# The MLP's second product by seven block products over pairs of k-tiles, and a phase table by Sin

## The chip, the cores and the metric

The program runs on one core of a Trainium2 chip. Its engines are TensorE (PE in the profile; the loading of its stationary operand is PEld), VectorE (DVE), ScalarE (ACT), GpSimd (POOL) and SyncE (SP), which here only issues DMAs. The metric is the device time of one execution in microseconds (us); lower is better. A measurement is the median of several executions.

## The reference

Two layers, each a token mixer with cross-attention into 256 memory tokens, and an MLP, with a layer norm behind each; 1024 tokens of width 1024. Layer 0 mixes by a gated delta rule, layer 1 by S5, a diagonal state-space layer. All inputs are float32. What the change touches is the MLP of both layers and a small table of S5:

```
f = jnp.square(jax.nn.relu(x @ mlp_w1[i])) @ mlp_w2[i]          # (1024,1024)@(1024,4096), then @(4096,1024)
x = layer_norm(DN_ALPHA * x + f, ln2_g[i], ln2_b[i])
...
abar_re, abar_im = mag * jnp.cos(a_im * dt), mag * jnp.sin(a_im * dt)   # S5: powers of these turn by a_im*dt each step
```

## The kernel before, in words

**Numbers.** A float32 factor is split into two parts of type fp32r: `hi`, a cast by ScalarE, and `lo`, the rest, a subtraction by VectorE (`split`, L528 for the subtraction). A product is three matmuls, hi·hi, hi·lo, lo·hi (`mm3`, L351 to L353), each 128 x 128 stationary against 512 moving columns into a PSUM bank.

**First product of the MLP** (`mlp_first`, `mlp_pair`). It is already done in blocks: the 32 tiles of 128 hidden units are taken as 16 pairs, tokens, inner dimension and the pair each halved, and seven block products (of 12 matmuls) replace eight, with sums before and behind. Their sums end in four hidden blocks of 128 units x 512 tokens per pair; `hidden` applies relu and square on ScalarE and stores the block in DRAM (`hd`). Operands of pair n+1 are made while pair n is multiplied (`mlp_weights`); their buffers have tags h1 to h5 with 5 to 9 slots each, and a split part waits until TensorE has left its slot.

**Second product** (`mlp_second`). Eight groups of four hidden tiles. A group loads and splits 4 tiles of hidden values (L676) and 4 of `w2` (L528), and then makes 16 blocks of 128 tokens x 512 columns; a block is 12 matmuls in a row into one bank (`tm`), and is added to `y` in SBUF (L698; by a ScalarE copy in the first group). Three banks take turns. In group 4 the residual is added (L702). In the last group each finished row of `y` gets its layer norm (`done`).

**S5's tables.** While layer 0's MLP runs, `side` does work that layer 1 will need, in steps `fb` 0 to 12: steps 1 to 4 make two of eight phase tables each (`s5_tables`, L1530, by doubling the range of angles seven times), and steps 5 to 12 each make two sets of matrices (`s5_mats`: on VectorE L1570 to L1572, on TensorE `pz` and `pg`). Steps 0 to 6 stood in the first product, 7 to 12 in the second.

**S5's front** (`s5_front`) is layer 1's mixer with its attention: `S` makes scores and their softmax, `T` transposes them, `V` multiplies by the values. Scores went to the banks `pi` and `sc`, one each.

**What sets the order.** At the end of tracing, `settle` lays the whole program out anew: it walks through all instructions with a price for each, due times from TensorE's row, and the slots of every tag, and fixes the order on each engine. A row that is late holds everything behind it on its engine.

## Time and profile before

| | |
|---|---|
| median of 3 runs | 2709.89 us (2707.24 to 2713.09) |
| profiled execution | 2711.34 us, its span 2709.6 us |
| TensorE busy | 2645.0 us, 98% of the span |
| VectorE busy | 1779.6 us, 66% |
| ScalarE, GpSimd busy | 1223.6 us and 355.9 us |
| data moved by DMA | 367.89 MB, mean 136 GB/s |
| layer 0, first product | from about 911 to 1172 us (some of it begins earlier) |
| layer 0, second product | from 1172 to about 1557 us |
| layer 1, first product, with the norm before it | about 2055 to 2350 us |
| layer 1, second product and end | about 2350 to 2709.6 us |

The span is the time from the first to the last instruction. A matmul's row shows its own duration; matmuls overlap, so durations do not add up to time. A row `start, duration, engine line op out<-in [idle <-releaser]` of a timeline names in brackets how long the engine had stood idle and what it then waited for. A row of windows gives, for a stretch, each engine's busy time with its instructions (x), the clock granted to TensorE (1.00 is full), and the DMA engines' share and rate.

### The profile page before, as it was taken

Reading aid. Unit: us, or ns where it says so; the run is one execution under the profiler, and the core shown is the slowest. Engines: PE = TensorE matmul, PEld = TensorE weight load, DVE = VectorE, ACT = ScalarE, POOL = GpSimd, SP = SyncE. Lnnn points to the kernel's source line nnn. Section 1 sums busy time; section 2 is a strip of 40 time slices with the busy share of each in tenths; the row PEclk is TensorE's granted clock in tenths of the full one; section 3 lists DMA queues with packets and bytes.
Section 4 is the critical chain, followed back from the end, with each engine's and each line's share of the span. In section 5 each row is a group of like instructions: output and inputs, shape, how many; then the busy total and the mean of one; then the engine's idle time right before and its main releaser. Section 6 shows DMA issues by size and latency. Waiting matters only on the chain.

```text
span 2709.6 us, 36841 instructions
## 1 busy us (share of the span) xinstructions
PE 2645.0 (98%) x13085; PEld 2183.8 (81%) x13085; DVE 1779.6 (66%) x3474; ACT 1223.6 (45%) x2773; POOL 355.9 (13%) x525
## 2 busy tenths in 40 slices
PE   8999999999999999999999999989999999999998
PEld 6888787888887788777777888878887888888887
DVE  6675757575769799746585766663768555535647
ACT  6666665654436544452222145553235545522210
POOL 1111212110003012201110122211011000000002
PEclk9999999999999999999999999999999999999999
DMA  5434444444423355463343186655323332533411
GB/s 197 130 118 124 125 113 120 122 134 139 152 78 132 123 164 165 148 208 120 128 146 120 70 247 195 194 183 179 121 71 131 107 117 101 194 113 127 154 63 62
DMA packets 233848, 367.89 MB, mean 136 GB/s; under 512 B 94224, under 2 KB 110816, under 8 KB 233664
## 3 DMA queue, kind: packets, MB, share of 16 engines
q1 hardware_dynamic: 212032, 308.40, 35.6%
q0 software_dynamic: 19328, 52.94, 6.5%
q10 hardware_dynamic: 2304, 4.20, 0.4%
q8 instruction: 103, 1.69, 0.3%
q14 instruction: 81, 0.66, 0.1%
HBM read 255.87 MB, written 109.54 MB: 135 GB/s over the span
## 4 chain that ended last, share of the span: by engine, by line
PE 76%; DVE 10%; ACT 5%; issue 3%; DMA 3%; POOL 1%; SPq 0%; POOLq 0%; ACTq 0%; DVEq 0%
PE tm L351 11%; PE tm L353 11%; PE tm L352 11%; PE pB L351 3%; PE pB L353 3%; PE pB L352 3%; PE iv L1035 2%; PE pC L351 2%; PE pC L353 2%; PE pC L352 2%; PE wi L353 2%; PE wi L351 2%; PE wi L352 2%; PE pA L351 2%; PE pA L353 2%
## 5 line engine op out<-in xcount | busy, mean ns | idle before, releaser
L351 PE MATMUL tm<-w2h,hk 128*128 128x512 f32 x1024 | 400.5, 391 | 0.0
L353 PE MATMUL tm<-w2h,hk 128*128 128x512 f32 x1024 | 399.4, 390 | 0.0
L352 PE MATMUL tm<-w2l,hk 128*128 128x512 f32 x1024 | 399.3, 390 | 0.0
L698 DVE TENSOR_TENSOR y<-tm,y 128x512 f32<-128x512 f32 x224 | 154.1, 688 | 212.4 <-PE tm L353 212.0
L527 ACT CAST w2h<-w2r 128x512 fp32r<-128x512 f32 x128 | 78.7, 621 | 375.3 <-PE tm L353 297.4
L351 PEld LDWEIGHTS tm<-w2h,hk 128*128 128x128 f32 x1024 | 192.2, 188 | 40.3 <-DVE y L698 0.3
L353 PEld LDWEIGHTS tm<-w2h,hk 128*128 128x128 f32 x1024 | 192.2, 188 | 39.9
L352 PEld LDWEIGHTS tm<-w2l,hk 128*128 128x128 f32 x1024 | 192.3, 188 | 39.3
L351 PE MATMUL wi<-xTh,wih 128*128 128x512 f32 x384 | 157.8, 411 | 0.0
L353 PE MATMUL wi<-xTh,wil 128*128 128x512 f32 x384 | 152.9, 398 | 0.0
L352 PE MATMUL wi<-xTl,wih 128*128 128x512 f32 x384 | 152.3, 397 | 0.0
L466 POOL TENSOR_SCALAR mv<-mv 128x1 f32<-128x1 f32 x32 | 26.2, 819 | 898.3 <-DVE mv L465 659.4
L1410 DVE TENSOR_TENSOR y<-tm,y 128x512 f32<-128x512 f32 x128 | 87.9, 688 | 59.5 <-PE tm L353 57.6
L528 DVE TENSOR_TENSOR w2l<-w2r,w2h 128x512 fp32r<-128x512 f32 x128 | 87.2, 689 | 50.9 <-PE tm L352 26.4
L676 DVE TENSOR_TENSOR hk<-hr,hk 128x512 fp32r<-128x512 f32 x128 | 83.4, 683 | 20.6 <-ACT hk L675 20.2
L353 PEld LDWEIGHTS wi<-xTh,wil 128*128 128x128 f32 x384 | 72.5, 189 | 13.9
L351 PEld LDWEIGHTS wi<-xTh,wih 128*128 128x128 f32 x384 | 72.8, 189 | 12.7 <-ACT qT L861 0.4
L352 PEld LDWEIGHTS wi<-xTl,wih 128*128 128x128 f32 x384 | 72.8, 190 | 12.3 <-issue 0.3
L535 ACT ACTIVATE u<-u 128x512 f32<-128x512 f32 x64 | 40.4, 631 | 89.2 <-DVE u L622 70.2
L675 ACT CAST hk<-hr 128x512 fp32r<-128x512 f32 x128 | 71.1, 617 | 14.7 <-DMA hr<-hd 13.1
L351 PE MATMUL tm<-ow,ok 128*128 128x512 f32 x160 | 63.5, 397 | 0.0
L353 PE MATMUL tm<-ow,ok 128*128 128x512 f32 x160 | 62.5, 391 | 0.0
(507 smaller groups left out, 7168.8 us busy)
## 6 DMA issues: line engine op xcount, KB each, us to landing
w2r<-in_w_dram SPq DMA_DIRECT2D x128, 256.0 KB, 3.5
hr<-hd SPq DMA_DIRECT2D x60, 512.0 KB, 4.5
w1r<-in_w_dram SPq DMA_DIRECT2D x40, 512.0 KB, 3.7
w1r<-in_w_dram SPq DMA_DIRECT2D x64, 256.0 KB, 4.5
hd<-u SPq DMA_DIRECT2D x64, 256.0 KB, 2.0
wir<-in_w_in_dram SPq DMA_DIRECT2D x24, 512.0 KB, 3.8
or<-in_w_o_dram SPq DMA_DIRECT2D x24, 512.0 KB, 3.4
or<-cat SPq DMA_DIRECT2D x24, 512.0 KB, 3.3
```

Of the source, the lines that this page charges most:

```text
L351: mm(ps, a[0], b[0], start=start, stop=False, skip_group_check=onto)
L352: mm(ps, a[0], b[1], start=False, stop=False, skip_group_check=onto)
L353: mm(ps, a[1], b[0], start=False, stop=stop, skip_group_check=onto)
L466: nc.gpsimd.tensor_scalar(mv[:, 2:3], mv[:, 1:2], 1e-5, None, op0=ALU.add)
L527: nc.scalar.copy(hi, s)
L528: nc.vector.tensor_tensor(lo, s, f32(hi), op=ALU.subtract)
L535: nc.scalar.activation(x, x, AF.Relu)
L675: nc.scalar.copy(hi, s)
L676: nc.vector.tensor_tensor(lo, s, f32(hi), op=ALU.subtract)
L698: nc.vector.tensor_tensor(o, ps, o, op=ALU.add)
L1035: nc.tensor.matmul(ps[:, t, :], a[:, t, :], b[:, t, :], start=True, stop=True)
L1410: nc.vector.tensor_tensor(y[c], ps, y[c], op=ALU.add)
```

## The change

**The second product.** Of the 16 pairs of hidden tiles, 14 are now multiplied in seven block products instead of eight: token halves by the pair's two tiles, the tiles by column halves. `mlp_round` takes 4, 5 and 5 pairs at once: for each of seven products in turn, it goes through the round's pairs and for each pair through four banks (`self.sets`, two sets of four that take turns), three matmuls per bank. Four of the products are added onto what the product two before left in the same banks; after each product the four banks are added to quarters of `y` (L755, L757), after the first to `x1` (L743, L745), which is added to three quarters at the end (L684). The last two pairs keep the old form (`mlp_last`).

**What that asks for.** The sums of hidden blocks are made once, in the first product (`hidden_sums`, L556, four per pair), and stored, so `hd` has seven blocks per pair. The sums of `w2` blocks are made in place (`source`, L693, four per pair). Each product of each pair splits both of its factors (`operand`, L764 for the subtraction).

**S5.** A phase table is now a remainder of turns, step times frequency, put through Sin on ScalarE; `s5_phases` shrinks accordingly. Steps 0 to 7 of the side work stand in the first product and 8 to 12 in the second, where the matrices use the bank set that is not in use. In `s5_front` the last scores go to the two `mm` banks, and `T` and `U` change places twice.

```diff
+SEVEN = 14
+SIDE = {3: 8, 7: 9, 10: 10, 14: 11, 17: 12}
...
-    def hidden(self, f, h, x):
+    def hidden(self, n, b, x):
 
...
-        nc.sync.dma_start(self.hd[f][:, h * HALF:(h + 1) * HALF], o)
+        nc.sync.dma_start(self.hd[n, b], o)
+        return o
+
+    def relu2(self, x):
+        self.nc.scalar.activation(x, x, AF.Relu)
+        self.nc.scalar.activation(x, x, AF.Square)
+
+    def hidden_sums(self, n, A11, A12, A21, A22):
+
+        if n >= SEVEN:
+            return
+        V = self.nc.vector
+        if A11 is None:
+            A11 = self.tile("h4", [P, HALF], F32, "hid")
+            self.nc.sync.dma_start(A11, self.hd[n, 0])
+        for b, o, x, z, op in ((3, A22, A21, A22, ALU.add), (5, A21, A11, A21, ALU.subtract),
+                               (4, A11, A22, A11, ALU.subtract), (6, A12, A12, A11, ALU.subtract)):
+            V.tensor_tensor(o, x, z, op=op)
+            self.nc.sync.dma_start(self.hd[n, b], o)
 
...
+        kept = []
+
         def second():
             if 1 in O:
                 go(2, a, False)
-                self.hidden(2 * n, 0, a)
+                kept.append(self.hidden(n, 0, a))
...
-        self.hidden(2 * n + 1, 1, u3)
+        self.hidden(n, 2, u3)
 
         def rest():
             go(3, c, False)
             V.tensor_tensor(u2, c, u2, op=ALU.add)
-            self.hidden(2 * n, 1, u2)
+            self.hidden(n, 3, u2) if n >= SEVEN else self.relu2(u2)
             go(4, b, False)
             V.tensor_tensor(p1, b, p1, op=ALU.add)
-            self.hidden(2 * n + 1, 0, p1)
+            self.hidden(n, 1, p1)
+            self.hidden_sums(n, kept[0] if kept else None, p1, u2, u3)
 
         held.append(rest)
 
...
-            if side and n % 2 == 0 and n:
-                side(n // 2 - 1)
+            for fb in {2: (0,), 4: (1,), 6: (2,), 8: (3,), 10: (4,), 11: (5,), 13: (6,), 15: (7,)}.get(n, ()) if side else ():
+                side(fb, ("pa",) * 4)
         self.finish(held)
...
     def mlp_second(self, i, xd, done, side):
 
...
+        self.sets = [("mm", "mm", "pi", "po"), ("pa", "pa", "pa", "sc")]
+        acc = {}
+        n0 = 0
+        for r, g in enumerate((4, 5, 5)):
+            self.mlp_round(i, r, range(n0, n0 + g), xd, acc, side)
+            n0 += g
+            self.sets.reverse()
+        y, x1 = acc["y"], acc["x1"]
+        for q in (1, 2, 3):
+            for t in range(4):
+                o = self.quarter(y, q, t)
+                self.nc.vector.tensor_tensor(o, o, x1[:, t], op=ALU.add)
+        self.mlp_last(i, y, done)
+
+    def quarter(self, y, q, t):
+        return y[4 * (q // 2) + t][:, (q % 2) * HALF:(q % 2 + 1) * HALF]
+
+    def mlp_round(self, i, r, pairs, xd, acc, side):
+        nc = self.nc
+        V = nc.vector
+        sub = lambda o, x, z: V.tensor_tensor(o, x, z, op=ALU.subtract)
+        L, R = slice(0, HALF), slice(HALF, 2 * HALF)
+        w2 = lambda n, q, o: nc.sync.dma_start(o, self.a["w2"][i, 2 * n + q])
+        r1, r2, t2 = self.quad(F32, "wr"), [], []
+        for j, n in enumerate(pairs):
+            if j == 4:
+                r1.append(self.tile("raw", [P, 1024], F32, "wr"))
+            w2(n, 0, r1[j])
+
+        def source(m, j, n):
+            if m == 1:
+                return r1[j][:, L]
+            if m == 6:
+                r2.append(self.tile("w1" if j < 4 else "raw", [P, 1024], F32, "wr"))
+                w2(n, 1, r2[j])
+                sub(r1[j][:, L], r1[j][:, R], r1[j][:, L])
+                t2.append(acc["x1"][:, 4 + j] if j < 4 else self.tile("h4", [P, HALF], F32, "t2"))
+                sub(t2[j], r2[j][:, R], r1[j][:, L])
+                return t2[j]
+            if m == 7:
+                sub(r1[j][:, R], r2[j][:, R], r1[j][:, R])
+                return r1[j][:, R]
+            if m == 4:
+                sub(r2[j][:, L], r2[j][:, L], t2[j])
+            return {2: r2[j][:, L], 5: r1[j][:, L], 4: r2[j][:, L], 3: r2[j][:, R]}[m]
+
+        left = {1: 0, 2: 1, 3: 6, 4: 2, 5: 3, 6: 4, 7: 5}
+        into = {1: None, 6: 1, 2: 0, 7: 3, 5: 3, 4: 2, 3: 1}
+        held = {}
+        for at, m in enumerate((1, 6, 2, 7, 5, 4, 3)):
+            own, onto = at % 2, m in (2, 7, 4, 3)
+            if not onto:
+                held[own] = [self.psum(t, f"q{m}") for t in self.sets[own]]
+            bank = held[own]
+            for j, n in enumerate(pairs):
+                s = self.tile("h3", [P, HALF], F32, "hr")
+                nc.sync.dma_start(s, self.hd[n, left[m]])
+                h = self.operand(s, "hk")
+                w = self.operand(source(m, j, n), "wk")
+                for t in range(4):
+                    c = slice(t * P, (t + 1) * P)
+                    self.mm3(bank[t], (h[0][:, c], h[1][:, c]), w, j == 0 and not onto, j == len(pairs) - 1, onto)
+                if j == 1 and side and 7 * r + at in SIDE:
+                    side(SIDE[7 * r + at], self.sets[1 - own])
+            if m == 1:
+                if r == 0:
+                    acc["x1"] = self.tile("xT", [P, 8, HALF], F32, "x1")
+                for t in range(4):
+                    o = acc["x1"][:, t]
+                    if r == 0:
+                        nc.scalar.copy(o, bank[t])
+                    else:
+                        V.tensor_tensor(o, bank[t], o, op=ALU.add)
+                continue
+            if "y" not in acc:
+                acc["y"] = self.quad(F32, "y") + self.quad(F32, "y")
+            for t in range(4):
+                o = self.quarter(acc["y"], into[m], t)
+                if r == 0 and m in (6, 2, 7, 4):
+                    x = self.tile("h4", [P, HALF], F32, "xr")
+                    q = into[m]
+                    nc.sync.dma_start(x, xd[4 * (q // 2) + t][:, (q % 2) * HALF:(q % 2 + 1) * HALF])
+                    V.scalar_tensor_tensor(o, x, ALPHA, bank[t], op0=ALU.mult, op1=ALU.add)
+                else:
+                    V.tensor_tensor(o, bank[t], o, op=ALU.add)
+
+    def operand(self, s, nm):
+        nc = self.nc
+        hi = self.tile("h2", [P, HALF], F32R, nm + "h")
+        lo = self.tile("h1", [P, HALF], F32R, nm + "l")
+        nc.scalar.copy(hi, s)
+        nc.vector.tensor_tensor(lo, s, f32(hi), op=ALU.subtract)
+        return hi, lo
+
...
+        nc.scalar.activation(W[2], W[2], AF.Exp)
+        V.tensor_tensor(W[1], W[1], W[2], op=M)
+        self.reduced(W[0], W[1])
...
     def s5_tables(self, c):
 
...
+        r, f = (self.tile("h5", [P, 4, P], F32, z) for z in ("tn", "tf"))
         cs = self.tile("gb", [P, 2, 4, P], F32, "cs")
...
+        scalar = lambda x, g: self.ph[x][:, 4 * c + g:4 * c + g + 1]
+        for g in range(4):
+            V.tensor_scalar(r[:, g], self.steps, scalar(0, g), 12582912.0, op0=ALU.mult, op1=ALU.add)
+        V.tensor_scalar(r, r, -12582912.0, None, op0=ALU.add)
+        for g in range(4):
+            V.scalar_tensor_tensor(f[:, g], self.steps, scalar(1, g), r[:, g], op0=ALU.mult, op1=ALU.subtract)
+        for g in range(4):
+            V.scalar_tensor_tensor(f[:, g], self.steps, scalar(2, g), f[:, g], op0=ALU.mult, op1=ALU.add)
+        V.tensor_scalar(f, f, 0.5, -0.5, op0=ALU.min, op1=ALU.max)
+        nc.scalar.activation(cs[:, 1], f, AF.Sin, scale=2 * math.pi)
+        nc.scalar.activation(r, f, AF.Sin, scale=-2 * math.pi)
+        nc.scalar.activation(f, f, AF.Abs)
+        nc.scalar.activation(cs[:, 0], f, AF.Sin, bias=self.quarter_turn, scale=-2 * math.pi)
...
         def S(h, hf):
-            p[hf] = self.attend_s(q[h][1][hf], kv, h, tags, banks)
+            p[hf] = self.attend_s(q[h][1][hf], kv, h, tags, ("mm", "mm") if h == 3 and hf else banks)
...
+            T(h, 0)
             U(m + 2, 0)
-            T(h, 0)
             V(h, 0)
+            T(h, 1)
             U(m + 2, 1)
-            T(h, 1)
             V(h, 1)
             read(m + 1)
```

**How the order moves.** VectorE in layer 1's first product, around the end of a pair. `pC` and `pB` are banks of pair n, `u` and `p` what is read out of them, `a4l`, `a1l`, `a2l` low parts for the next pairs. Before:

```order
L622 TENSOR_TENSOR u_3635_19941<-pC_19975,u_3635_19941 128x512
L528 TENSOR_TENSOR a4l_19910<-w1r_19875,a4h_19909 128x512
L625 TENSOR_TENSOR p_3633_19926<-pB_19928,p_3633_19926 128x512
L528 TENSOR_TENSOR a1l_20033<-w1r_20022,a1h_20032 128x512
L528 TENSOR_TENSOR a2l_20045<-w1r_20022,a2h_20044 128x512
```

and now:

```order
L644 TENSOR_TENSOR u_3927_20707<-pC_20748,u_3927_20707 128x512
L556 TENSOR_TENSOR u_3930_20789<-u_3927_20707,u_3930_20789 128x512
L530 TENSOR_TENSOR a4l_20676<-w1r_20641,a4h_20675 128x512
L556 TENSOR_TENSOR u_3927_20707<-hid_20773,u_3927_20707 128x512
L647 TENSOR_TENSOR p_3925_20692<-pB_20694,p_3925_20692 128x512
L556 TENSOR_TENSOR hid_20773<-u_3930_20789,hid_20773 128x512
L530 TENSOR_TENSOR a1l_20806<-w1r_20795,a1h_20805 128x512
```

The three L556 rows are sums of hidden blocks of pair n, and stand ahead of `a1l`; the first of them needs the relu and square of `u`, which ScalarE makes after L644.

VectorE where layer 0's first product ends and the second begins. Before (`w2l` belongs to the second product's first group):

```order
L622 TENSOR_TENSOR u_2154_11649<-pC_11651,u_2154_11649 128x512
L528 TENSOR_TENSOR w2l_11759<-w2r_11756,w2h_11758 128x512
L528 TENSOR_TENSOR w2l_11765<-w2r_11762,w2h_11764 128x512
L625 TENSOR_TENSOR p_2151_11586<-pB_11636,p_2151_11586 128x512
L528 TENSOR_TENSOR w2l_11771<-w2r_11768,w2h_11770 128x512
```

and now, around the last read of `pB` (`wr` are halves of `w2`, `x` holds sums of them for the second block product, `H` and `cw` are S5's matrices):

```order
L647 TENSOR_TENSOR p_2107_11389<-pB_11439,p_2107_11389 128x512
L693 TENSOR_TENSOR wr_11610<-wr_11610 128x512 x2
L1668 TENSOR_TENSOR H_2233_11995<-co_11485,pw_9028 128x512
L1669 TENSOR_TENSOR cw_11996<-co_11485,pw_9028 128x512
L1670 TENSOR_TENSOR H_2233_11995<-H_2233_11995,cw_11996 128x512
L1670 TENSOR_TENSOR H_2117_11506<-H_2117_11506,cw_11507 128x64
L1670 TENSOR_TENSOR H_2128_11545<-H_2128_11545,cw_11546 128x64
L693 TENSOR_TENSOR x_2162_11707<-wr_11722,wr_11610 128x512
L693 TENSOR_TENSOR x_2162_11707<-wr_11748,wr_11610 128x512
L693 TENSOR_TENSOR x_2162_11707<-wr_11774,wr_11610 128x512
L764 TENSOR_TENSOR wkl_11727<-x_2162_11707,wkh_11726 128x512
```

Three sums, each with a `wr` tile of its own, now stand ahead of the low part that the second block product needs first.

TensorE at the last scores of S5's front (`sc`). Before:

```order
L352 MATMUL sc_16914<-kv_15053,qh_16837 128x256
L353 MATMUL sc_16914<-kv_15053,ql_16838 128x256
L1707 MATMUL py_16962<-s5t_14888 128x128
L351 MATMUL sc_16930<-kv_15053,qh_16884 128x256
L352 MATMUL sc_16930<-kv_15053,qh_16884 128x256
```

and now:

```order
L354 MATMUL sc_17009<-kv_15148,qh_16932 128x256
L355 MATMUL sc_17009<-kv_15148,ql_16933 128x256
L353 MATMUL sc_17025<-kv_15148,qh_16979 128x256
L354 MATMUL sc_17025<-kv_15148,qh_16979 128x256
L1805 MATMUL py_17057<-s5t_14983 128x128
L355 MATMUL sc_17025<-kv_15148,ql_16980 128x256
```

The rows stand nearly alike; `sc_16930` took the bank that the first of these scores had held, `sc_17025` has a bank `mm` of its own.

More of the change, by code (lines that the diff above doesn't have):

```diff
@@ new lines, in s5_phases @@
+        V.tensor_tensor(W[1], W[1], W[2], op=M)
+        self.reduced(W[0], W[1])
+        room = self.tile("h5", [P, HALF], F32, "ph")
+        self.ph = ph = [room[:, 128 + 32 * x:160 + 32 * x] for x in range(3)]
+        V.tensor_scalar(W[1], W[1], 8 / (2 * math.pi), None, op0=M)
+        V.tensor_scalar(W[0], W[1], 12582912.0, -12582912.0, op0=A_, op1=A_)
+        V.tensor_tensor(ph[0], W[1], W[0], op=S_)
+        V.tensor_scalar(ph[1], ph[0], 96.0, -96.0, op0=A_, op1=A_)
+        V.tensor_tensor(ph[2], ph[0], ph[1], op=S_)
@@ L1523, in s5_tables @@
+        self.steps = n = room[:, 0:P]
+        V.memset(n[:, 0:1], 0.0)
+        for k in range(7):
+            V.tensor_scalar(n[:, 1 << k:2 << k], n[:, 0:1 << k], float(1 << k), None, op0=A_)
+        self.quarter_turn = room[:, 224:225]
+        V.memset(self.quarter_turn, math.pi / 2)
     def s5_tables(self, c):
         nc = self.nc
-        G = nc.gpsimd
         V = nc.vector
-        M, A_, S_ = ALU.mult, ALU.add, ALU.subtract
-        g = lambda o, x, y, op: V.tensor_tensor(o, x, y, op=op)
@@ L1610, in s5_mats @@
         dd = self.dd(8 * m + 4 * b)
-        pz = self.psum("pa", "pz", (P, 4, 8, 16))
+        pz = self.psum(banks[0], "pz", (P, 4, 8, 16))
         for g in range(4):
```

159 lines of the change are left out of this document (54 added, 105 removed).

## The prediction

> **What bounds the kernel now.** I read the page's first part and its costliest groups, then a table of windows by stage, then TensorE's and VectorE's timelines at a few places. The page puts TensorE at 98%, and its largest groups are the second product's matmuls, with no idle time ahead of them:
>
> ```profile
> PE 2645.0 (98%) x13085; PEld 2183.8 (81%) x13085; DVE 1779.6 (66%) x3474; ACT 1223.6 (45%) x2773; POOL 355.9 (13%) x525
> ...
> L351 PE MATMUL tm<-w2h,hk 128*128 128x512 f32 x1024 | 400.5, 391 | 0.0
> L353 PE MATMUL tm<-w2h,hk 128*128 128x512 f32 x1024 | 399.4, 390 | 0.0
> L352 PE MATMUL tm<-w2l,hk 128*128 128x512 f32 x1024 | 399.3, 390 | 0.0
> L698 DVE TENSOR_TENSOR y<-tm,y 128x512 f32<-128x512 f32 x224 | 154.1, 688 | 212.4 <-PE tm L353 212.0
> ```
>
> So 3072 matmuls stand there (3 x 1024), and those who read their banks wait for TensorE, not it for them. The durations overlap, so the price of a matmul is the step from one start to the next. Two rows of the timeline, the first and the last of 28 in a row:
>
> ```profile
> 2449.65 0.39 PE L353 MATMUL tm<-w2h,hk 128*128 128x512 f32 x1
> ...
> 2455.77 0.39 PE L353 MATMUL tm<-w2h,hk 128*128 128x512 f32 x1
> ```
>
> 6.12 us over 27 steps is 0.2267 us each. The stages, in the order layer 0's first product, its second, layer 1's first, its second with the end (columns: stretch, its length, busy time of PE, PEld, DVE, ACT, POOL, clock, DMA):
>
> ```profile
> 911.00:1172.00 261.00, 254.05 (x1127) 201.87 (x1126) 227.99 (x726) 130.83 (x226) 53.22 (x113) 0.99 0.48 159
> 1172.00:1522.00 350.00, 350.00 (x1652) 278.06 (x1651) 215.39 (x398) 91.37 (x162) 42.89 (x69) 1.00 0.40 130
> 2055.00:2350.00 295.00, 289.76 (x1282) 236.46 (x1282) 173.87 (x274) 149.66 (x259) 4.44 (x4) 1.00 0.36 123
> 2350.00:2709.60 359.60, 350.96 (x1549) 290.27 (x1547) 194.29 (x290) 78.26 (x139) 15.06 (x16) 0.99 0.33 113
> ```
>
> In both second products TensorE is the whole time; VectorE is at 62% and 54%. In layer 0's first product VectorE stands at 87% already, and TensorE idles 7 us. That is where the change could hurt.
>
> **The change part by part.** *Matmuls.* A pair of hidden tiles was 2 tiles x 16 blocks x 3 = 96 matmuls and becomes 7 x 4 x 3 = 84. Fourteen pairs in two layers save 14 x 2 x 12 = 336, at 0.2267 us: **-76.2 us**. (By the rows' durations of 0.39 us it would be 131 us; that counts the overlap twice.) The Trainium skill, "TensorE: Matmul & The Clock Gate", section "Wait — 56ns, not 53.3ns?", gives 215.7 ns from start to start at 512 columns; by that the estimate is 72.5 us, and the rows of this trace, 226.7 ns, decide.
>
> *VectorE.* Its rows of 128x512 follow each other faster than they last, too:
>
> ```profile
> 1270.79 0.69 DVE L1570 TENSOR_TENSOR H<-co,pw 128x512 f32<-128x512 f32 x1
> ...
> 1272.59 0.69 DVE L1572 TENSOR_TENSOR H<-H,cw 128x512 f32<-128x512 f32 x1
> ```
>
> Three steps in 1.80 us, 0.60 each. A second product had 256 such rows per layer (128 splits, 112 adds, 16 residuals). Now it has 196 + 16 splits, 56 sums of `w2`, 56 + 16 adds and 16 of them fused with the residual, 8 + 12 for `x1`, 16 `w2` splits of the last group: 392. That is 136 more, +82 us. A first product gets 56 sums, +34 us. The phase tables give some back in layer 0:
>
> ```profile
> 0.00:2709.60 2709.60, 61.93 (x336) 1.00 0.43 136
> ...
> L1189 DVE SCALAR_TENSOR_TENSOR R<-ks,scr,mix 128x128 f32<-128x128 f32 x56 | 19.5, 348 | 18.6 <-PE ks L1187 18.5
> ...
> L1549 DVE TENSOR_SCALAR ns<-cs 128x512 f32<-128x512 f32 x8 | 3.5, 433 | 0.1
> ...
> L1588 DVE TENSOR_SCALAR s5b<-s5b,sg 128x128 f32<-128x128 f32 x8 | 2.4, 304 | 5.4 <-DMA s5b<-in_b_dram 5.4
> ```
>
> The first row is L1530 alone, 61.9 us; with L1549 65 us go. Each of eight tables now has four rows like L1588, two like L1549 and eight like L1189: 4.9 us, 39 in all, so -26. A side step of S5 costs about (215 - 256 x 0.60) / 6 = 10 us of VectorE, and one moves from the second product into the first. Layer 0: first product 228 + 34 - 26 + 10 = 246 us in 261 (94%), second 215 + 82 - 10 = 287 in 350 - 38 = 312 (92%). Layer 1: 208 in 295 (70%), 276 in 322 (86%). TensorE still covers all of it, barely in layer 0; without that cover the excess counts in full. In a round of five pairs without side work VectorE has 118 rows, 71 us, against 420 matmuls, 95 us.
>
> *ScalarE* gets 72 more casts and copies per second product, at most 72 x 0.63 = 45 us on 91 in 312: hidden by TensorE. *DMA*: 42 more stores and 42 more loads of 256 KB per layer, 44 MB on 368; mean 136 GB/s becomes about 156, where one stretch carried 247 (below): hidden, except as a latency.
>
> *Waits.* A wait of TensorE costs more than itself, because the matmuls behind it run at half pace for a while:
>
> ```profile
> 1163.69 0.50 PE L351 MATMUL pB<-xB,a4h 128*128 128x512 f32 x1 [0.78 <-DVE u L616]
> ...
> 1165.78 0.70 PE L351 MATMUL pC<-xB,s4h 128*128 128x512 f32 x1 [1.14 <-DVE u L617]
> 1166.28 0.63 PE L352 MATMUL pC<-xB,s4h 128*128 128x512 f32 x1
> ...
> 1168.84 0.62 PE L352 MATMUL pC<-xB,s4h 128*128 128x512 f32 x1
> ```
>
> Six steps in 2.56 us, 0.427 each instead of 0.227: 1.9 us of waits and about eight slow matmuls, 1.6 us more.
>
> S5's front has the largest wait outside the start:
>
> ```profile
> PE sc L351 <- ACT p L1309: 4.5, 1, 4.5
> ...
> 1783.49 0.28 PE L353 MATMUL sc<-kv,ql 128*128 128x256 f32 x1
> ...
> 1788.51 0.58 PE L351 MATMUL sc<-kv,qh 128*128 128x256 f32 x1 [4.51 <-ACT p L1309]
> ...
> 1750.00:1800.00 50.00, 43.13 (x244) 37.72 (x242) 39.66 (x81) 31.80 (x60) 5.14 (x4) 0.93 0.59 177
> ```
>
> The second pair of scores waits for a bank that the first softmax is still reading; then the clock is low (0.93 of 50 us is 3.5 us). With a bank `mm` it need not wait: at best -4.5 - 3.5 = -8 us. But the softmax still takes its time, and its reader, the transpose, is late next: in the new order only some 16 small and nine wide matmuls stand between. If that wait grows by as much, the other end is +4. I take **-5**, nearer the whole gain, since some work does stand between.
>
> First product, own pairs (ten per layer that have sums and no early start). The three sums now stand ahead of `a1l`:
>
> ```profile
> L535 ACT ACTIVATE u<-u 128x512 f32<-128x512 f32 x64 | 40.4, 631 | 89.2 <-DVE u L622 70.2
> ...
> 2201.67 0.39 PE L351 MATMUL pB<-xB,a4h 128*128 128x512 f32 x1
> ...
> 2208.02 0.40 PE L353 MATMUL pA<-xB,a1l 128*128 128x512 f32 x1
> ...
> 2201.87 0.69 DVE L622 TENSOR_TENSOR u<-pC,u 128x512 f32<-128x512 f32 x1 [0.56 <-PE pC L353]
> ...
> 2207.16 0.69 DVE L528 TENSOR_TENSOR a1l<-w1r,a1h 128x512 fp32r<-128x512 f32 x1 [1.50 <-PE pC L352]
> ```
>
> From L622's start: 0.69, two ScalarE rows 1.26, then five VectorE rows at 0.60 = 4.95, so `a1l` could start at 2206.8; TensorE leaves its slot only at about 2207.1 anyway. That leaves 0.3 us, less a few hand-overs. What is late next is `a1l` and TensorE behind it. Between 0 and 0.8 us a pair (half a microsecond late and some slow matmuls), 0 to +16 in all; nearer the first, since the rows nearly fit: **+4**.
>
> Layer 0's pairs 11 to 15 now hold three side steps: 3 x 10 + 5 pairs x 20 rows x 0.60 = 90 us of VectorE in 5 x 84 x 0.2267 = 95 of TensorE. A stall there like the one at 1165 costs 3.5; three of them would be 10: **+3**, 0 to +10.
>
> The step to the second product. Three sums wait for `w2` tiles whose slots are freed by the last block product of the first stage. They are needed 48 x 0.2267 = 10.9 us later:
>
> ```profile
> 1150.00:1200.00 50.00, 48.08 (x212) 37.73 (x211) 29.13 (x59) 27.59 (x50) 6.85 (x11) 0.97 0.71 247
> ...
> 2500.00:2600.00 100.00, 100.00 (x443) 82.81 (x442) 60.69 (x94) 24.35 (x43) 0.00 (x0) 1.00 0.39 131
> ...
> w1r<-in_w_dram SPq DMA_DIRECT2D x40, 512.0 KB, 3.7
> ```
>
> At 247 GB/s the third 512 KB tile lands 3.7 + 2 x 2.1 = 7.9 us later, and sum, cast and split add 1.8: 9.7, in time. At 131 GB/s it is 13.3, 2.4 late, with slow matmuls 4 to 6 per layer. 0 to +12, taken **+2**.
>
> Sum: -76.2 - 5 + 4 + 3 + 2 = -72.2. The profiled execution took 2711.34 us, 1.74 around its span of 2709.6, and stands 1.45 above the median: 2711.3 - 72.2 - 1.45 = **2638 us**. The end of the program (adds and norms of the last rows) keeps its order.
>
> **The rivals.** *VectorE sets the pace in layer 0.* For it: 94% and 92% asked of an engine with a fixed order that reached 87% in its densest stage. If 87% is all it can do, the first product takes 246 / 0.87 = 283 (+22) and the second 287 / 0.87 = 330 (+18); with the +3 replaced, 2638 + 37 = 2675. Against it: side work has no near date and can fill gaps.
>
> *The bank sets are handed over late, and it is slower.* At each of the 42 products TensorE goes to the other set of four banks; four reads of 0.69 us must have left it. If it had to wait, the matmuls behind would run at 0.427 us as above. A stall like that at 1165 (3.5 us) at each boundary gives 42 x 3.5 = 147 us, 2785 us; from 72 / 42 = 1.7 us per boundary it is slower than before. Against it: the set was filled one whole product earlier, 48 or 60 matmuls, 10.9 or 13.6 us. The Trainium skill's "TensorE: Matmul & The Clock Gate", section "A second HAM failure mode: psum-queue depth-cycling", warns of a matmul loop that cycles through banks, whose small idle gaps keep dropping the clock. No row here shows that: where three banks take turns now, from 2500 to 2600 us, the clock is 1.00.
>
> *A change of bank costs a matmul its overlap.* There will be 2352 / 3 = 784 changes where 224 stood. At 0.39 - 0.2267 = 0.163 us each, +91, 2729 us, slower; from 0.13 us it decides. Against it stand rows that change bank with every matmul, at 0.23 us:
>
> ```profile
> 12.83 0.39 PE L351 MATMUL wi<-xTh,wih 128*128 128x512 f32 x1
> 13.06 0.40 PE L775 MATMUL ba<-xTl,wbah 128*16 128x512 f32 x1
> 13.29 0.39 PE L352 MATMUL wi<-xTl,wih 128*128 128x512 f32 x1
> ```
>
> *The change does not do what it says* in one part: the new tables shorten VectorE's work, not TensorE's, and are worth nothing where TensorE sets the time. That lies in the forecast.
>
> **How the numbers follow.** Forecast 82%: 2638, its own range 2626 (S5's whole 8 us, no new stall) to 2656 (half of the stalls' upper ends). VectorE's pace 12%: 2675. Late hand-over 4%, cost of a bank change 2%. The range is 2624 to 2666: it leaves out most of the rivals and the forecast's far ends. About 0.2% (5 us) can be told from no change here. Faster 0.94 (forecast and VectorE's pace), slower 0.05 (the last two, less a part of the bank's that stays under 0.13 us), same 0.01.
>
> **What would show it.** TensorE's count falls by 336 and the starts in the new groups are 0.227 us apart. TensorE's idle time in both second products stays under 5 us, while VectorE's share there is near 90%. The wait of `sc` on ScalarE is gone; a longer one before the transposes `pT` would take its place. New waits of `pA` on `a1l` in layer 1 would be the sums of the hidden blocks; a wait of the second block product on a low part, the loads. If starts in the new groups are further apart, or the granted clock falls there, the forecast is wrong in its main term.

## The result, and the profile after

The changed kernel takes 2643.65 us (median, 2640.99 to 2645.90) against 2708.86 us of the kernel before, measured beside it: a ratio of 0.9757, 95% interval 0.9740 to 0.9773. It is faster by 65.2 us where 72.2 were forecast; the time lies in the range of 2624 to 2666, 5.65 us above the forecast of 2638.

The first part and the costliest groups of the page of the changed kernel (line numbers are now those of the changed kernel: `mm3` is L353 to L355, `operand` L763 and L764):

```profile
span 2644.2 us, 37215 instructions
...
PE 2574.2 (97%) x12749; PEld 2119.7 (80%) x12749; DVE 1938.9 (73%) x3560; ACT 1319.4 (50%) x2943; POOL 349.8 (13%) x509
...
L354 PE MATMUL q<-wkl,hkh 128*128 128x512 f32 x784 | 306.0, 390 | 0.4 <-DVE wkl L764 0.4
L353 PE MATMUL q<-wkh,hkh 128*128 128x512 f32 x784 | 306.3, 391 | 0.0
L355 PE MATMUL q<-wkh,hkl 128*128 128x512 f32 x784 | 306.0, 390 | 0.0
...
L757 DVE TENSOR_TENSOR y<-q,y 128x512 f32<-128x512 f32 x112 | 71.9, 681 | 0.0
```

TensorE has 12749 matmuls, 336 fewer than 13085. The 2352 of the new rounds (`q`) waited 0.4 us in all, and none of it for a bank. The old-form group behind them waited for a bank once per layer, 0.4 and 0.9 us (`tm` on the last additions to `y`, L757). The pace of the new rounds, by the first and the last of 37 rows of TensorE's timeline:

```profile
1299.79 0.39 PE L353 MATMUL q<-wkh,hkh 128*128 128x512 f32 x1
...
1307.94 0.39 PE L353 MATMUL q<-wkh,hkh 128*128 128x512 f32 x1
```

8.15 us over 36 steps: 0.226 us each, as before.

The stages, cut at the first matmul of each (for the first products, the first `pB`). First the windows of the kernel before, then of the changed one, in the order layer 0's first product, its second, S5's front, layer 1's first product, its second with the end (columns as in the prediction: stretch, length, PE, PEld, DVE, ACT, POOL, clock, DMA share and GB/s):

```profile
864.90:1172.30 307.40, 300.43 (x1326) 239.13 (x1326) 262.67 (x784) 154.36 (x268) 53.22 (x113) 0.99 0.47 156
1172.30:1557.20 384.90, 384.90 (x1825) 307.21 (x1824) 249.74 (x447) 97.50 (x173) 51.56 (x84) 1.00 0.38 126
1557.20:1893.60 336.40, 322.37 (x1714) 274.48 (x1714) 197.48 (x356) 166.53 (x290) 72.46 (x86) 0.99 0.65 200
2068.00:2352.60 284.60, 283.69 (x1246) 232.59 (x1246) 165.11 (x260) 144.38 (x246) 0.00 (x0) 1.00 0.35 121
2352.60:2709.60 357.00, 348.36 (x1537) 288.11 (x1536) 192.04 (x286) 76.58 (x136) 15.06 (x16) 0.99 0.33 112
```

```profile
865.50:1182.20 316.70, 305.87 (x1362) 240.65 (x1362) 261.50 (x583) 165.60 (x293) 55.82 (x101) 0.99 0.59 196
1182.20:1526.00 343.80, 342.98 (x1621) 273.33 (x1620) 311.96 (x557) 140.62 (x246) 46.10 (x80) 1.00 0.51 168
1526.00:1859.80 333.80, 323.91 (x1714) 275.13 (x1713) 196.50 (x357) 166.28 (x291) 71.26 (x85) 0.98 0.66 201
2033.80:2322.60 288.80, 285.27 (x1247) 232.36 (x1247) 194.36 (x309) 141.79 (x241) 0.00 (x0) 1.00 0.48 168
2322.60:2644.20 321.60, 310.86 (x1369) 256.40 (x1367) 261.82 (x413) 120.78 (x213) 12.88 (x16) 0.99 0.46 152
```

The two second products gain 41.1 and 35.4 us. Layer 0's includes the 36 matmuls of the one side step that went to its first product. Layer 0's first product loses 9.3 us, layer 1's 4.2, S5's front gains 2.6, and the rest is within 1 us. VectorE stands at 312 of 344 us in layer 0's second product (91%, forecast 92%) and 262 of 322 in layer 1's (81%, forecast 86%), and TensorE covers it: 0.8 us idle in layer 0, and in layer 1 10.7 us, 8.6 before, nearly all of it at the program's end. In layer 0's first product VectorE's busy time has not grown at all (262.7 and 261.5 us): the new tables give back what the sums cost.

Where the first products lose time, by TensorE's waits over the whole program:

```profile
PE pB L353 <- DVE u L638: 5.9, 4, 3.3
...
PE pB L353 <- ACT s2h L529: 3.4, 2, 1.7
PE wg L354 <- DVE xTl L1832: 2.7, 2, 2.5
...
PE pA L355 <- DVE a1l L530: 2.0, 3, 0.9
```

The wait of `sc` on the softmax (4.5 us) is gone, and `wg` now waits 2.5 us for `xTl` further on in the same stage. The longest new one is in layer 0's first product; VectorE's rows ahead of it, then TensorE's:

```profile
1062.17 0.69 DVE L556 TENSOR_TENSOR p<-p,hid 128x512 f32<-128x512 f32 x1 [2.74 <-DMA hd<-p]
1063.09 0.29 DVE L1678 TENSOR_TENSOR co<-s5b,pw 128x128 f32<-128x128 f32 x1 [0.22 <-DMA tabd<-cs]
1065.33 0.29 DVE L1686 TENSOR_SCALAR s5b<-s5b,sg 128x128 f32<-128x128 f32 x1 [1.94 <-DMA s5b<-in_b_dram]
...
1066.46 0.68 DVE L638 TENSOR_TENSOR u<-pB,p 128x512 f32<-128x512 f32 x1
...
1067.20 0.80 PE L353 MATMUL pB<-xB,a4h 128*128 128x512 f32 x1 [3.31 <-DVE u L638]
1067.79 0.63 PE L354 MATMUL pB<-xB,a4h 128*128 128x512 f32 x1
...
1072.48 0.63 PE L353 MATMUL pC<-xB,s4h 128*128 128x512 f32 x1
```

The last hidden sum is written over the block `p`, which is still being stored, so it waits for that store; behind it a coefficient row of S5 waits for its load; and only then comes the row (L638) that reads the bank TensorE wants next. The wait of 3.31 us is followed by eleven steps of 0.426 us (4.69 us between the last two rows). Layer 1, which has no rows of S5 there, shows waits behind sums and stores too, smaller: 0.93 us behind the last sum, and 1.70 us where three sums, and a slot whose block is still being stored, stand ahead of the row that `s2h` needs.

### The profile page after: what moved, and what is told of

It is laid out like the page before. It is cut to its first block, busy times and chain, and to the rows that moved or that the text cites. A ratio compares the mean times of both kernels' runs of the same rounds, so it can differ in the third digit from the quotient of the medians.

```text
span 2644.2 us, 37215 instructions
## 1 busy us (share of the span) xinstructions
PE 2574.2 (97%) x12749; PEld 2119.7 (80%) x12749; DVE 1938.9 (73%) x3560; ACT 1319.4 (50%) x2943; POOL 349.8 (13%) x509
## 4 chain that ended last, share of the span: by engine, by line
PE 51%; DVE 5%; issue 4%; ACT 2%; DMA 1%; POOL 0%; POOLq 0%; SPq 0%; DVEq 0%; ACTq 0%
PE q L354 6%; PE q L353 6%; PE q L355 6%; PE pB L353 2%; PE pB L355 2%; PE pB L354 2%; PE tm L353 2%; PE tm L355 2%; PE tm L354 2%; PE pC L353 1%; PE pC L355 1%; PE pC L354 1%; PE pA L353 1%; PE pA L355 1%; PE pA L354 1%
## 5 line engine op out<-in xcount | busy, mean ns | idle before, releaser
L354 PE MATMUL q<-wkl,hkh 128*128 128x512 f32 x784 | 306.0, 390 | 0.4 <-DVE wkl L764 0.4
L353 PE MATMUL q<-wkh,hkh 128*128 128x512 f32 x784 | 306.3, 391 | 0.0
L355 PE MATMUL q<-wkh,hkl 128*128 128x512 f32 x784 | 306.0, 390 | 0.0
L763 ACT CAST wkh<-wr 128x512 fp32r<-128x512 f32 x168 | 104.9, 625 | 235.3 <-PE q L354 187.4
L354 PEld LDWEIGHTS q<-wkl,hkh 128*128 128x128 f32 x784 | 147.2, 188 | 31.3 <-DVE wkl L764 1.1
L353 PEld LDWEIGHTS q<-wkh,hkh 128*128 128x128 f32 x784 | 147.2, 188 | 31.1 <-ACT wkh L763 0.5
L355 PEld LDWEIGHTS q<-wkh,hkl 128*128 128x128 f32 x784 | 147.2, 188 | 30.5
L764 DVE TENSOR_TENSOR wkl<-wr,wkh 128x512 fp32r<-128x512 f32 x168 | 115.6, 688 | 72.8 <-issue 52.9
L353 PE MATMUL wi<-xTh,wih 128*128 128x512 f32 x384 | 157.7, 411 | 0.0
L355 PE MATMUL wi<-xTh,wil 128*128 128x512 f32 x384 | 153.0, 398 | 0.0
L764 DVE TENSOR_TENSOR hkl<-hr,hkh 128x512 fp32r<-128x512 f32 x196 | 134.0, 684 | 1.2 <-ACT hkh L763 1.2
L1507 DVE TENSOR_TENSOR y<-tm,y 128x512 f32<-128x512 f32 x128 | 87.9, 688 | 59.4 <-PE tm L355 57.6
L763 ACT CAST hkh<-hr 128x512 fp32r<-128x512 f32 x196 | 120.8, 616 | 0.0
L355 PEld LDWEIGHTS wi<-xTh,wil 128*128 128x128 f32 x384 | 72.4, 189 | 13.8
L353 PEld LDWEIGHTS wi<-xTh,wih 128*128 128x128 f32 x384 | 72.8, 189 | 12.8 <-ACT qT L958 0.4
L757 DVE TENSOR_TENSOR y<-q,y 128x512 f32<-128x512 f32 x112 | 71.9, 681 | 0.0
L353 PE MATMUL tm<-ow,ok 128*128 128x512 f32 x160 | 63.5, 397 | 0.0
L355 PE MATMUL tm<-ow,ok 128*128 128x512 f32 x160 | 62.5, 391 | 0.0
```

The lines of the kernel that those rows point to most:

```text
L353: mm(ps, a[0], b[0], start=start, stop=False, skip_group_check=onto)
L354: mm(ps, a[0], b[1], start=False, stop=False, skip_group_check=onto)
L355: mm(ps, a[1], b[0], start=False, stop=stop, skip_group_check=onto)
L757: V.tensor_tensor(o, bank[t], o, op=ALU.add)
L763: nc.scalar.copy(hi, s)
L764: nc.vector.tensor_tensor(lo, s, f32(hi), op=ALU.subtract)
```

## The experiments

The questions: is the gain the matmuls alone; what did each of the smaller edits bring; where are the 7 us that are missing; and was one of the rivals near? Times are medians of five rounds (three for the bank and the doubled rows), to be held against 2643.65 us of the changed kernel and 2708.4 to 2709.4 us of the kernel before, which ran beside each. The medians rest on four to eight executions that spread by 1 to 6 us, so differences below about 3 us are not told apart.

### The S5 parts alone, and the change without the new tables

On the kernel before, tables and S5's front from the change:

```diff
 # kernel before
+    def reduced(self, k, x): ...
-    def s5_phases / s5_tables / s5_front      (doubling of angles, old order)
+    def s5_phases / s5_tables / s5_front      (turns through Sin, new order and banks)
```

> The kernel before with the S5 parts of the change alone: tables by Sin, short phase step, new order and banks in S5's front; the second product keeps its eight groups. By the forecast's terms (front -5, tables 0) it takes 2704 us, and the wait of sc on the softmax (4.5 us) is gone. If the front is worth only what the stage of the two kernels differs by (-2.6), 2706 us. Rival: the tables free VectorE in layer 0's first product (about 26 us less there) and TensorE's 11 us of idle time in that stage shrink with it: 2699 us or less.

On the changed kernel, the old tables:

```diff
 # changed kernel
-    def s5_phases / s5_tables                 (turns through Sin)
+    def s5_phases / s5_tables                 (doubling of angles, L1530 of the kernel before)
```

> The changed kernel with the old phase tables (doubling of angles on VectorE). If tables are worth nothing because TensorE sets the time, 2641 to 2646 us, as with the change. Rival: in the changed kernel VectorE stands at 274 of 332 us in layer 0's first product; with about 26 us more it is at 300 and, since side steps crowd pairs 11 to 15, its stalls grow: 2649 to 2659 us.

Measured: the S5 parts alone take 2714.18 us, 1.0024 of before (1.0013 to 1.0034), 5.3 us *slower*. The changed kernel without the new tables takes 2670.10 us, 0.9861 of before (0.9847 to 0.9874), 26.4 us slower than with them. So the new second product with the old tables gains 38.8 us, the S5 parts by themselves lose 5.3, and together they gain 65.2: the effects do not add up, by 31.7 us. All expectations on tables were missed but the rival's direction for the second kernel, whose size (5 to 15 us) was too small. Layer 0's first product with the old tables, its window:

```profile
865.10:1204.50 339.40, 313.74 (x1362) 244.80 (x1361) 292.01 (x853) 150.51 (x264) 58.14 (x120) 0.96 0.55 182
```

and TensorE's longest waits there (us in all, times, longest):

```profile
PE pB L353 <- DVE u L638: 7.5, 3, 5.4
PE pA L355 <- DVE a1l L530: 3.6, 3, 2.7
PE pC L355 <- DVE s1l L530: 2.7, 3, 1.4
```

VectorE has 30.5 us more to do (292.0 against 261.5), the stage lasts 22.7 us longer, and TensorE waits all over it for VectorE, at a clock of 0.96.

In the kernel with the S5 parts alone VectorE has 32 us less in that stage, and yet the stage is 4.7 us longer, here its window and then TensorE's longest waits:

```profile
865.90:1178.00 312.10, 299.83 (x1327) 239.27 (x1327) 230.27 (x519) 167.43 (x294) 52.21 (x97) 0.98 0.47 153
```

```profile
PE pA L353 <- DVE a1l L528: 4.9, 5, 2.5
PE pg L1622 <- DVE G1T L1573: 4.3, 1, 4.3
```

From VectorE's timeline and then TensorE's, the longest wait for `a1l`:

```profile
1010.46 0.68 DVE L528 TENSOR_TENSOR a1l<-w1r,a1h 128x512 fp32r<-128x512 f32 x1
...
1011.20 0.50 PE L353 MATMUL pA<-xB,a1l 128*128 128x512 f32 x1 [2.51 <-DVE a1l L528]
```

The row of `a1l` starts at 1010.46, though its operand was cast by 1006.9; VectorE was busy from 1003.4 on, and from 1005.0 16 rows of a table (128 columns each) stand ahead of it in the order. Less work on the engine, but laid at a worse place. Why the layout put it there is not settled; one guess is tried below.

### Sums left out, with the new and with the old tables

```diff
 # hidden_sums, changed kernel / changed kernel with the old tables
-            V.tensor_tensor(o, x, z, op=op)
             self.nc.sync.dma_start(self.hd[n, b], o)
```

> The changed kernel without the four sums of hidden blocks per pair (the four blocks are stored as they are, so the loads and stores stay, and the second product multiplies other numbers): 56 rows of VectorE less in each first product, 34 us. By the forecast's terms for them (+4 and +3) 2637 us. By the stages of the two profiles (layer 0's first product 9.9 us longer, of which 39 matmuls of the side step some 3 us, layer 1's 4.2 us longer) up to 11 us less, 2633 us. Rival: VectorE sets the pace of layer 0's first product, and then TensorE's 11 us of idle time there go as well: 2629 us or less.

> The changed kernel with the old phase tables and without the sums of hidden blocks. The changed kernel with the old tables alone took 2670.1 us, its VectorE 292 of 339 us in layer 0's first product. If VectorE's load is the cause, the 34 us that the sums leave there bring back nearly all: 2637 to 2645 us, VectorE near 260 of 310 us. Rival: something else in the old tables (GpSimd's part, their stores, their place) costs the 26 us: about 2660 us.

Measured: 2642.52 us and 2641.57 us. With the old tables, leaving out the sums brings back 28.5 us; with the new ones, 1.1 us. So VectorE's load was the cause of the old tables' price, as expected, and nothing else in them. (With the sums go their waits for stores as well, but with the old tables VectorE waits only 0.2 us for a store at L556, in the changed kernel 5.3.) Layer 0's first product, the window of the first and then of the second kernel:

```profile
865.90:1174.30 308.40, 302.60 (x1362) 240.26 (x1362) 230.24 (x527) 166.06 (x293) 55.41 (x103) 0.99 0.59 199
```

```profile
865.50:1181.10 315.60, 306.92 (x1363) 242.04 (x1363) 262.90 (x793) 152.50 (x267) 56.68 (x119) 0.98 0.59 196
```

With the rows above this is a curve of VectorE's work against the stage's length, for the same matmuls (1362, side work included):

| VectorE busy in layer 0's first product | length of the stage | kernels |
|---|---|---|
| 230 us | 308.4 us | no sums |
| 261.5 to 262.9 us | 311.1 to 318.2 us | nine kernels, the change at 316.7 |
| 292 us | 339.4 us | old tables |

The first 32 us cost 3 to 10, by one kernel at 230 us. The S5 parts alone, also at 230 us and with 36 small matmuls fewer, took 312.1, so this part of the curve is hardly told from scatter. The next 30 cost 21 to 28. The bend lies above 262 us, close to where the change stands; with loads at three places only, it is not known better.

For the sums the expectation of 2629 to 2637 us was missed: in the profiled executions the stage gave 8.3 us, layer 1's first product 3.7 (285.1 us in its window), but layer 0's second product, whose order had shifted, took 7.9 back. TensorE's waits in that stage:

```profile
PE pg L1718 <- DVE G1T L1669: 2.9, 2, 2.0
PE pz L1710 <- DVE H L1669: 2.2, 1, 2.2
```

These are the side work's matmuls, waiting for VectorE. With the old tables and no sums the same stage shows 0.4 us of `pg` and lasts 344.2 us. The price of the sums in layer 1, where no side work runs, is clean: 3.7 us with the new tables, 3.6 with the old. This stage repeats well: from its first `pB` to the next product it takes 288.1 to 289.2 us in the ten kernels that have the sums and the new second product.

### S5's front as before

```diff
 # s5_front, changed kernel
-            p[hf] = self.attend_s(..., ("mm", "mm") if h == 3 and hf else banks)
+            p[hf] = self.attend_s(..., banks)
-            T(h, 0)
             U(m + 2, 0)
+            T(h, 0)
             V(h, 0)
-            T(h, 1)
             U(m + 2, 1)
+            T(h, 1)
```

> The changed kernel with the old order and banks in S5's front. By the forecast's term it is 5 us slower than the change, 2648.7 us; by the difference of that stage in the two profiles 2.6 us, 2646.3 us. Rival: the wait was only moved to the products behind, and the edit is worth nothing, 2643.7 us. The wait of sc on the softmax, about 4.5 us, is back in all three.

Measured: 2643.38 us, no difference from the change. TensorE's waits in S5's front, in this kernel and then in the changed one (whose wait for `xTl` is in the list above as well):

```profile
PE sc L353 <- ACT p L1406: 4.5, 1, 4.5
PE pv L353 <- ACT pTh L1423: 2.8, 4, 0.9
PE wg L354 <- DVE xTl L1832: 1.9, 2, 1.0
```

```profile
PE wg L354 <- DVE xTl L1832: 2.7, 2, 2.5
PE pv L353 <- ACT p L1406: 1.4, 1, 1.4
```

The stage takes 335.0 us with the old front and 333.8 with the new. The wait of 4.5 us goes, but `pv` waits for the softmax and `wg` longer for `xTl`, and the loss of clock behind a wait stays, and is no smaller: from 1745 to 1780 us the clock is 0.90 with the old front and 0.85 in the changed kernel. The rival, that the wait only moved, stands.

This kernel also tells how much a single profile is worth. Up to S5's front its order on every engine is that of the changed kernel, but for one MEMSET of VectorE near 602 us, yet layer 0's first product took 313.1 us in its profiled execution and 316.7 in the change's. There VectorE waited 0.5 us for S5's coefficients and not 1.94, and TensorE 1.18 us behind it and not 3.31.

### Every matmul another bank

```diff
 # mlp_round
-                for t in range(4):
-                    self.mm3(bank[t], (h[0][:, c], h[1][:, c]), w, ...)
+                for u, v in ((0, 0), (0, 1), (1, 0)):
+                    for t in range(4):
+                        nc.tensor.matmul(bank[t], h[u][:, c], w[v], ...)
```

> The changed kernel, in the rounds of the second product a bank changed with every matmul (the same part product for the four banks in turn) instead of with every third: 2352 changes of bank instead of 784. If a change of bank costs nothing, 2641 to 2647 us, starts stay 0.227 us apart and the clock 1.00. The rival with 0.163 us a change: 1568 more changes cost 256 us, 2900 us. A clock that drops with cycling banks would show below 1.00 from 1200 to 1500 us.

Measured: 2646.51 us (2644.74 to 2648.54), 2.9 us above the change, which the spread does not tell from nothing. Two rows of TensorE's timeline, each of four matmuls into four banks:

```profile
1299.96 1.07 PE L735 MATMUL q<-wkh,hkl 128*128 128x512 f32 x4
...
1307.21 1.07 PE L735 MATMUL q<-wkl,hkh 128*128 128x512 f32 x4
```

32 steps in 7.25 us, 0.227 us each, at a clock of 1.00. The change of bank is free to 2.9 us / 1568 = 0.002 us, against the rival's 0.163. The Trainium skill, "TensorE: Matmul & The Clock Gate", section "A second HAM failure mode: psum-queue depth-cycling", has a kernel whose clock drops when it cycles through banks; with no gap between the matmuls, no such drop is seen here.

### A second row for each low part of w2

```diff
 # operand
         nc.vector.tensor_tensor(lo, s, f32(hi), op=ALU.subtract)
+        if nm == "wk":
+            nc.vector.tensor_tensor(lo, s, f32(hi), op=ALU.subtract)
```

> The changed kernel, the low part of every w2 operand in the rounds computed twice: 98 more rows of 128x512 on VectorE per second product, 59 us at 0.60 us each. In the changed kernel VectorE stands at 312 of 344 us in layer 0's and 262 of 322 in layer 1's second product. If TensorE sets the time until VectorE is full: layer 0 becomes 371 us (+27), layer 1 stays at about 322 (+0 to +5), in all 2671 to 2676 us. Rival: an engine with a fixed order reaches only 87%: layer 0 takes 371 / 0.87 = 426 us (+82), layer 1 321 / 0.87 = 369 (+47), in all 2773 us.

Measured: 2687.90 us, 44.3 us above the change, between the two expectations (+27 to +32, and +129). The windows of layer 0's and layer 1's second products:

```profile
1179.50:1564.20 384.70, 352.61 (x1621) 277.79 (x1620) 366.08 (x652) 140.16 (x246) 46.75 (x80) 0.95 0.46 149
2362.60:2686.90 324.30, 310.87 (x1369) 256.47 (x1367) 314.91 (x510) 120.91 (x213) 11.02 (x16) 0.99 0.46 151
```

TensorE's longest wait in the first of them:

```profile
PE pz L1714 <- DVE dd L1817: 26.7, 3, 10.3
```

and from VectorE's timeline the row that it waited for the first time:

```profile
1234.18 0.20 DVE L1817 TENSOR_TENSOR dd<-ident,dsk 16x64 f32<-16x64 f32 x1
```

VectorE reaches 95% and 97%, not 87%: layer 1, with no side work, loses 2.7 us for 98 more rows, as it should if TensorE sets the time until VectorE is full. Layer 0 loses 41. There TensorE stands 8 to 10 us at three of the side steps: a matmul `pz` of the step needs `dd`, a row of 0.20 us that stands behind all that VectorE owes in its fixed order.

### The side work shared otherwise

```diff
 # side_back
-SIDE = {3: 8, 7: 9, 10: 10, 14: 11, 17: 12}
+SIDE = {3: 7, 6: 8, 10: 9, 13: 10, 17: 11, 20: 12}
-            {2: 0, 4: 1, 6: 2, 8: 3, 10: 4, 11: 5, 13: 6, 15: 7}     # pair: side step
+            {2: 0, 4: 1, 6: 2, 8: 3, 10: 4, 12: 5, 14: 6}
 # side_even
+            {1: 0, 3: 1, 5: 2, 7: 3, 9: 4, 11: 5, 13: 6, 15: 7}
```

> The changed kernel with the side work as it was shared before: steps 0 to 6 in layer 0's first product (pairs 2, 4, 6, 8, 10, 12, 14), 7 to 12 in its second. If the crowded pairs 11 to 15 cost what the forecast put down (+3), 2640.7 us; by the slope that the sums showed (8.2 us of time for some 31 us of VectorE in that stage) 10 us of VectorE less give 2.7 us, 2641 us. VectorE rises from 312 to about 322 of 347 us in layer 0's second product. Rival: there the side work's matmuls then wait for VectorE as they do with every w2 low part computed twice (26.7 us in three waits): 2649 us or more.

> The changed kernel with the eight side steps of layer 0's first product behind every second pair (1, 3, ..., 15) instead of three in pairs 11 to 15. If crowding costs, as the forecast put down (+3), 2640.7 us. If only VectorE's whole load in the stage counts, which stays, 2643.7 us, and the stage lasts 312 to 317 us as in the profiles so far.

Measured: 2657.85 us with six steps in the second product, 14.2 us above the change; 2642.97 us (2642.35 to 2643.69) with even spacing, no difference. With a step moved back, layer 0's first product is 8.3 us shorter but its second 19.5 us longer; some 3 us of either are the 36 small matmuls of the step. The window of the second, and then TensorE's waits in it:

```profile
1175.10:1538.40 363.30, 354.16 (x1657) 279.33 (x1658) 323.09 (x577) 145.07 (x253) 51.62 (x84) 0.98 0.49 160
```

```profile
PE tm L353 <- ACT w2h L529: 5.1, 2, 4.7
PE q L353 <- ACT wkh L763: 3.5, 2, 2.5
```

VectorE has 11 us more, as expected, and is at 89%. The rival's sign holds, at another place: the operands of the last, old-form group are late, and ScalarE, which casts them, waits 7.5 us for their loads. Part of that is probably where this kernel's last step stands (product 20, right ahead of that group); no run moves it alone. So the 14 us are the price of this sharing, not of a sixth step at any place. The step in the first product was well placed. Even spacing shows that crowding in pairs 11 to 15 costs nothing that can be told.

### Three other orders of the same work

The last hidden sum to a slot of its own; DMAs reckoned longer by the layout; VectorE's small rows reckoned dearer:

```diff
 # sum_apart: hidden_sums
-    (6, A12, A12, A11, ALU.subtract)      # in place
+    (6, None, A12, A11, ALU.subtract)     # o = self.tile("h5", [P, HALF], F32, "p6")
 # dma_later: the call of settle
-    margin=0.15, late=0.7
+    margin=0.15, late=1.4
 # small_rows_dearer: price, VectorE
-    t = 0.07 + ...
+    t = (0.07 if big > 128 else 0.14) + ...
```

> The changed kernel, the last of the four hidden sums written to a slot of its own instead of over the block that is still being stored. My reading of the new profile: VectorE waits up to 2.7 us there for the store, and behind it stands the sum that frees a bank for the fourth block product; TensorE waited 3.3 us in layer 0 and 0.9 in layer 1, each with slow matmuls behind. So 4 to 9 us faster than the change, 2635 to 2640 us, and VectorE's wait for a store of the hidden block is gone. Rival: the three sums ahead of the next pair's operands cost the time, not the store: no difference, 2642 to 2645 us.

> The changed kernel, laid out with every DMA reckoned 0.7 us longer (late 1.4 instead of 0.7); the work is the same, only the order on the engines changes. If TensorE's stalls in layer 0's first product come from VectorE rows that stand in the order ahead of a DMA's landing (the last hidden sum on a store, the coefficients of S5 on a load), the stage gets 3 to 5 us shorter: 2639 to 2641 us. Rival: with VectorE this full another row waits instead: 2642 to 2646 us, and the waits have other names.

> The changed kernel, laid out with VectorE's rows of up to 128 columns reckoned 0.07 us longer (0.14 instead of 0.07 us beside the part by columns), nearer to the 0.27 us step that they show; the work is the same. If table rows that take longer than planned push a1l and the sums back, the stage gets 2 to 4 us shorter: 2640 to 2642 us. Rival: no difference, 2642 to 2646 us, since what counts is VectorE's whole load there.

Measured: 2647.89 us (2646.39 to 2648.93), 2650.64 us (2649.95 to 2651.22) and 2647.09 us (2644.97 to 2647.98): the first two slower than the change by 4 and 7 us, the third not faster. All three gains were missed. In the first, VectorE's wait for the store is gone, as meant, and the row of S5's `H` is late instead. TensorE's waits in layer 0's first product:

```profile
PE pz L1713 <- DVE H L1672: 5.2, 1, 5.2
PE pB L353 <- ACT s2h L529: 2.3, 1, 2.3
```

The stage took 318.2 us. With the longer DMAs it took 316.5, the waits had other names (`pA` on `a1l` 3.3, `pz` on `H` 2.3), and S5's front became 5 us longer. With the dearer rows it took 311.1, and the gain did not show in the median. The store was a link of one stall, not the cause of the loss; at 262 us of VectorE's work in that stage another row takes its place. That under-priced small rows push the others back is not shown.

No version tried that computes the same result is faster than the change beyond what can be told; the even spacing and the old order of S5's front are its equals.

## Why the prediction was right, and where it was not

**Matmuls, -76.2.** Right in mechanism and size. 336 matmuls went, the starts stayed 0.226 us apart, and the two second products together are 76.5 us shorter. Some 3 us of that are the side step's small matmuls, which layer 0's first product has now, so the term itself is nearer -73; layer 1's second product gave 35.4 where 38.1 were forecast; 2.1 us of the rest are idle time of TensorE, 1.0 of it behind the last matmul of the program and 0.9 where the old-form group waits for a bank.

**Tables, "worth nothing on PE".** This step failed. They are worth 26.4 us in the changed kernel. The prediction's own sum of VectorE's work had the tables' -26 us in it, and without them would have come to 272 us in 261; the text priced the tables at nothing all the same, because it asked what they save with TensorE as the bound, and not what would happen to the sums without them. The sum of 72.2 came out near since it counted sums and tables together against VectorE's cover: the total is no evidence for the statement about the tables alone.

**VectorE's shares.** 92% and 86% forecast in the second products, 91% and 81% measured. The forecast's count of 392 rows has the 16 splits of the last group twice; there are 376, 10 us less, and VectorE's work grew by 62 us in layer 0 and 70 in layer 1 where 72 and 82 were forecast. In layer 0's first product 94% were forecast, of the 261 us from 911 on; over the whole stage the same terms make 281 us, 89% of its 316.7, and 261.5 us, 83%, came. The tables freed 32 us and not 26, the sums took 31 and not 34, the moved step 7 and not 10, and seven operand rows of the second product, 4 us, no longer stand in the stage; some 3 us stay unexplained.

**S5's front, -5.** Wrong: undoing it changes nothing (2643.38 us). The prediction's other end, "that wait grows by as much", is what happened in part: `pv` waits 1.4 us for the softmax, `wg` 2.5 for `xTl`, and the clock is low all the same (0.85 over 35 us, 0.90 with the old front). The stage's window is 2.6 us shorter, but the median is not.

**First product, own pairs, +4.** Under-sized, and the place was wrong. The forecast put 2 us on each layer; leaving out the sums gives 3.7 in layer 1. `a1l` is not late there. In layer 1 the time goes in two early pairs: the row for `s2h` stands behind three sums and a store, and the read of a bank behind the last sum, which waits for a store. That the sums are written in place over blocks that are being stored was in the diff, and the prediction did not look at it.

**Layer 0's crowded pairs, +3.** Not shown: even spacing gives the same time. What lengthened that stage (9.3 us, some 3 of them the moved matmuls) stays in part open: VectorE's work there is that of the kernel before, and at this work the nine kernels took 311.1 to 318.2 us, by their orders and from execution to execution. Leaving out the sums gave 8.3 us of its length.

**Step to the second product, +2.** At its low end: TensorE waits 0.2 us there in each layer.

**The rivals.** VectorE's pace, priced by a ceiling of 87%, did not come. The ceiling is no general one: the second products reached 95% and 97%. But in layer 0's first product, the stage from which it was read, no run went above 86% of the whole stage: with the old tables 292 us of work took 339.4 us, and 292 / 0.87 is 336. And its mechanism decides as soon as VectorE gets 30 us more in layer 0's first product (old tables) or 54 in its second (doubled rows), so 12% was not too much for a change that lies this near. Hand-over of the bank sets: no `q` waited for a bank, and `tm` behind the rounds 0.4 and 0.9 us. Change of bank: 0.002 us, no more than the spread. The forecast's bound for that, rows that changed bank with every matmul at 0.23 us, was the right row to look at.

**The missing 7 us.** By the stages: 2.7 in layer 1's second product, 2.4 in S5's front (-2.6 for -5), 1.2 in layer 1's first product (4.2 for 3, its shares of the sums and of the step to the second product); layer 0 came out as forecast (9.3 us in its first product, some 3 of them the moved matmuls, for 6). Layer 1's two figures are backed by repetition: its first product took 288.1 to 289.2 us in ten kernels against 284.6 and 284.7 in the two with the old second product, its second 321.6 to 322.1 in all that leave it as in the change, against 357.0 in those two. The front's share is backed by a run of its own. Layer 0's first product is known to no better than 4 us.

## What to carry to other kernels

An edit that shortens the engine which is *not* the bound can be worth nothing, or cost a little, alone, and pay for another edit that loads that engine: price such edits together, at the load that the engine will have, and run each alone only to learn where the bend is. Where an engine works in a fixed order near its limit, look at what stands behind each row that waits for a DMA, and at results written in place over a block that is still being stored. Mending one such stall, at that load, only moved it.

## What the runs showed of the hardware that was not expected

The slow matmuls behind the wait of 3.31 us have a low granted clock, 0.52 in the window of the changed kernel there:

```profile
1066.00:1072.00 6.00, 4.80 (x11) 3.80 (x12) 3.15 (x8) 1.26 (x2) 2.17 (x5) 0.52 0.85 310
```

A wait of 1.70 us in layer 1 cost three steps of some 0.32 us, and then the pace was 0.23 again; in the kernel with the old front, the wait of 1.18 us was followed by steps of 0.34 and 0.24 us. The Trainium skill, "TensorE: Matmul & The Clock Gate", section "Wait — 56ns, not 53.3ns?", gives 426.7 ns from start to start at 512 columns while the array is cold, that is at its lower clock, and the steps of 0.426 us agree. Its section "HAM oscillation — how this bites in real kernels" names idle gaps above some 3.4 us as the danger; in the kernel before, two waits of 0.78 and 1.14 us, 2 us apart, were followed by six steps of 0.427, so the measurement decides: shorter waits close together can be enough. Why these were and the single 1.70 us was not, no run here shows.

The same order of the same work took 316.7 and 313.1 us in one stage of two executions, with a load that VectorE waited for 1.4 us longer in one of them: the length of that stage in a single profile is known to about 4 us here, while layer 1's first product repeats within 1.1 us.
